# Last attention pair: block transfers over two queues with diagonal copies on GpSimd, one head weighted on ScalarE, maxima exchanged in another PSUM bank

## The chip, the cores and the metric

The kernel runs on one core of one Trainium2 chip. The metric is device microseconds of one execution; a kernel's time is the median of several. Engines are named as the profile names them: PE (TensorE matmul), PEld (its weight load), DVE (VectorE), ACT (ScalarE), POOL (GpSimd), SP (SyncE, which here only issues transfers); SPq and ACTq are the transfers that SP and ACT issue.

## The reference

Two layers over 512 tokens of width 1024: an attention mixer, a gated feed-forward, an mLSTM mixer and another feed-forward. The change touches the attention mixer alone. It has 8 heads of width 128 and three groups of queries, keys and values (window and dilation 128/1, 512/4, 2048/16):

```python
for g, (window, dilation) in enumerate(DIL_CONFIGS):
    q = apply_partial_rope(proj[:, :, g, 0], positions) * scale
    k = apply_partial_rope(proj[:, :, g, 1], positions)
    v = proj[:, :, g, 2]
    o, lse = dilated_window_attention(q, k, v, window, dilation)   # softmax within a group
    ...
wts = jax.nn.softmax(jnp.stack(lses), axis=0)                      # softmax over the groups
o = jnp.einsum('gbsh,gbshd->bshd', wts.astype(xn.dtype), jnp.stack(outs))
return o.reshape(B, S, ATTN_WIDTH) @ w_out
```

## The kernel before

All products of float32 data are made of three matmuls: each operand is split into a high part (ACT, names ending in `_h`) and a rest (DVE, `_l`), and high x high, low x high and high x low are summed in PSUM. PE runs nearly without a break through the whole program, and the other engines prepare its operands.

Attention goes by pairs of heads (`attention_pair(pr)`, pr 0 to 3; tiles of pair 3 begin with `a3`, those of pair 2 with `a2`; pair 3 is heads 6 and 7). Each pair has these steps:

- projections of q and k, then `scores0` and `scores12`: scores, masks with row maxima on DVE, exponentials on ACT. The result for head i is tile `p[i]` (`a3p`), 15 blocks of 128x128.
- `joint`: the groups hold their tokens in two orders, so each row's maximum and sum must be brought to the other order. `exchange` does this with one matmul into a PSUM tile `xps` (`a3xps`). `joint` then makes the weights `cf` (`a3cf`).
- `weigh(i)`: eight multiplications of blocks of `p[i]` by a column of `cf`, on DVE.
- `transposes(i)`: one DVE instruction transposes all 32x32 blocks within `p[i]` into `t` (`a3pB`). What is left of a 128x128 transpose is to move block row b of partition group a to block row a of group b.
- For pairs 0 to 2 that move goes through DRAM on POOL's queue (`bring(i)`), hidden behind the next pair. For pair 3 (`end`) there is no next pair: 16 transfers a head of 32x480 go straight from `a3pB` to `a3pT`, head 6's alternately on ACT and SP, head 7's all on SP.
- `values(i)`: 30 recorded matmuls of `a3pT` with the values give the head's output in PSUM (`a3o`), which is split into `ao_h` and `ao_l` for the output projection.

PSUM tiles come from four tags, each a ring of buffers: "s" (2), "o" (2), "acc" (3) and "t" (1). Scores, `xps` and the heads' outputs use "o". A tile waits until the one that held its buffer has been read.

The last pair's work is interleaved by hand with the output projection (`awo`, in four column chunks c of 256, each in two row chunks `_k0` and `_k1`); `run` keeps the PE instructions of a step together and in order. On PE the order is: `awo` chunk 0, scores of pair 3, chunk 1, head 4's values (`a2o`), the exchange, head 5's values, chunk 2, then the parts of all chunks that need heads 4 and 5, head 6's values between the second and the third of them, head 7's values, and the parts that need heads 6 and 7. The weights of chunk 2's second row chunk are split on ACT (L207) and DVE (L208) behind the transfers that ACT issues.

Of the kernel before, what the change touches and what calls it, by code (L numbers as in the profile page):

```python
# [11 lines left out]
F32 = mybir.dt.float32  # L12
F32R = mybir.dt.float32r
I32 = mybir.dt.int32
AF = mybir.ActivationFunctionType
ALU = mybir.AluOpType
AX = mybir.AxisListType
P = 128
# [5 lines left out]
HEADS = 8  # L24
# [46 lines left out]
def tile_hybrid_dilated_attn_mlstm(  # L71
# [4 lines left out]
    nc = tc.nc  # L76
# [3 lines left out]
    def pool(stack, name, **kw):  # L80
        return stack.enter_context(tc.tile_pool(name=name, bufs=1, **kw))
# [4 lines left out]
    ps = pool(ctx, "psum", space=bass.MemoryType.PSUM)  # L86
# [51 lines left out]
    def defer(n, fn):  # L138
        later.append((tick[0] + n, next(order), fn))
# [36 lines left out]
    def fenced():  # L176
        return tc.issue_after(fence[0]) if fence[0] is not None else nullcontext()

    def acc_tile(name):
        return ps.tile([P, 512], F32, tag="acc", name=name, bufs=3)  # L180
# [163 lines left out]
    with ExitStack() as actx:  # L344
# [3 lines left out]
        R = 32  # L348
# [12 lines left out]
        ang, n, sn, cs = (boot[:, 0, i * P:(i + 1) * P] for i in range(4))  # L361
# [28 lines left out]
        def tok_tile(name):  # L390
            return ap.tile([P, 2, SEQ], F32, tag="qk", name=name, bufs=6)
# [16 lines left out]
        xps = {}  # L408
# [286 lines left out]
        def columns(c0):  # L695
# [4 lines left out]
                            lambda i, tb, n=n: v_all[1 + n][i][tb]) for n in range(2)]  # L700
# [35 lines left out]
        def o_head(k):  # L736
            return v_all[0][:, :, k * P:(k + 1) * P]

        def attention_pair(pr):
            nm = "a%d" % pr  # L740
# [7 lines left out]
            end = pr == HEADS // 2 - 1  # L748
            pts, vt, weight = {}, [], []

            def score_bank(i, name):
                return ps.tile([P, 512], F32, tag="so"[i], name=name, bufs=2)
# [23 lines left out]
            def scores12(qk1, qk2):  # L776

                for i in range(2):
                    for g, (q, k) in ((1, qk1), (2, qk2)):
                        sp = score_bank(i, "%ss%d" % (nm, g))  # L780
                        for c in range(4):
                            sl = slice(c * P, (c + 1) * P)
                            nc.tensor.matmul(sp[:, sl], q[:, i, sl], k[:, i, sl], start=True, stop=True)
                        for c in range(4):
                            sl = slice(c * P, (c + 1) * P)
                            nc.vector.tensor_tensor_reduce(
                                p12[i][:, 4 * (g - 1) + c, :], sp[:, sl], mask_causal if g == 1 else mask_dil,
                                1.0, -3e38, op0=ALU.add, op1=ALU.max, accum_out=mx[:, g - 1, i, c:c + 1])
                    exponentials(1, i)
# [20 lines left out]
            def exchange():  # L810

                ex = ap.tile([P, 2, 2, 2, 4, 4], F32, tag="ex", name=nm + "ex")
                for st in range(2):
                    nc.vector.tensor_tensor(
                        ex[:, st].rearrange("p o i b c -> p (o i b) c"),
                        own[:, st].rearrange("p o i b -> p (o i b)").unsqueeze(2).to_broadcast([P, 16, 4]),
                        mask_part.unsqueeze(1).to_broadcast([P, 16, 4]), op=ALU.mult)
                xps = ps.tile([P, 512], F32, tag="o", name=nm + "xps", bufs=2)
                nc.tensor.matmul(xps[:, :P], perm, ex.rearrange("p s o i b c -> p (s o i b c)"), start=True, stop=True)
                ex2 = ap.tile([P, 8, 4, 4], F32, tag="ex2", name=nm + "ex2")  # L820
                nc.vector.tensor_tensor(
                    ex2, xps[:, :P].rearrange("p (s b c) -> p s c b", b=4, c=4),
                    mask_part.unsqueeze(1).unsqueeze(1).to_broadcast([P, 8, 4, 4]), op=ALU.mult)
                ex4 = ex2.rearrange("p (s o i) c b -> p s o i c b", s=2, o=2)
                for o in range(2):
                    nc.vector.tensor_reduce(oth[:, :, 1 - o], ex4[:, :, o], axis=AX.X, op=ALU.add)
# [18 lines left out]

            def weigh(i):
                cf4 = weight[0]
                for b in range(4):
                    pb = max(2 * b - 1, 0)
                    blk = p0[i][:, pb:2 * b + 1, :].rearrange("p a b -> p (a b)")  # L850
                    nc.vector.tensor_scalar(blk, blk, cf4[:, 0, i, b:b + 1], None, op0=ALU.mult)
                for c in range(4):
                    blk = p12[i].rearrange("p (g c) k -> p c g k", g=2)[:, c]
                    nc.vector.tensor_scalar(blk, blk, cf4[:, 1, i, c:c + 1], None, op0=ALU.mult)

            def transposes(i):


                t = ap.tile([P, 4, 15, R], F32, tag="p", name=nm + "pB", bufs=3)
                nc.vector.transpose(t.rearrange("p b n i -> p n b i"), p[i])  # L860
                if end:
                    pt = pts[i] = ap.tile([P, 4, 15, R], F32, tag="pt", name=nm + "pT", bufs=2)
                    for n in range(16):
                        a, b = n // 4, n % 4
                        (nc.sync if n % 2 or i else nc.scalar).dma_start(pt[R * b:R * (b + 1), a], t[R * a:R * (a + 1), b])
                    return
                d = pts[i] = dp.tile([4, R, 4, 15 * R], F32, tag="d", name=nm + "pD", bufs=2)
                for a in range(4):
                    nc.gpsimd.dma_start(d.rearrange("b j a x -> a j b x")[a],
                                    t[R * a:R * (a + 1)].rearrange("p b n i -> p b (n i)"))  # L870

            def bring(i):
                if end:
                    return
                pt = ap.tile([P, 4, 15, R], F32, tag="pt", name=nm + "pT", bufs=2)
                nc.gpsimd.dma_start(pt.rearrange("p a n i -> p (a n i)"), pts[i].rearrange("b j a x -> (b j) (a x)"))
                pts[i] = pt
# [20 lines left out]
            qks = []  # L898
            for g in range(3):
# [3 lines left out]
                for part in range(2):  # L903
                    t = tok_tile("%sg%d_%s" % (nm, g, "qk"[part]))
# [30 lines left out]
                    values_stage()  # L935
                if g == (2 if pr == 0 else 0):
                    defer(1 if pr == 0 else RUN_AT[0], lambda: run(lambda: scores0(*qks[0])))
            turn = ((lambda: weigh(0), lambda: transposes(0), lambda: bring(0), lambda: weigh(1), lambda: transposes(1),
                     lambda: bring(1)) if pr == HEADS // 2 - 1 else
                    (lambda: weigh(0), lambda: transposes(0), lambda: weigh(1), lambda: transposes(1),  # L940
                     lambda: bring(0), lambda: bring(1)))
            later_runs = ((lambda: scores12(*qks[1:]),), (joint, *turn))
            if pr < 2:
                later_runs += ((lambda: values(0), lambda: values(1)),)
            v1 = v_all[1 + pr // 2]
            vt.extend(lambda c, i, g=g: v1[g][c][:, (pr % 2 * 2 + i) * P:(pr % 2 * 2 + i + 1) * P] for g in range(2))
            if pr == HEADS // 2 - 1:
                return [lambda fns=fns: run(*fns) for fns in later_runs], values
            for at, fns in zip(RUN_AT[1:], later_runs):
                defer(at, lambda fns=fns: run(*fns))  # L950
# [4 lines left out]
        for pr in range(HEADS // 2):  # L955
            last_runs, values_of = attention_pair(pr)
# [5 lines left out]
        def heads_split(*ks):  # L962
            for k in ks:
                split_act(blocks4(pair[0][k]), blocks4(pair[1][k]), o_head(k), None)
# [7 lines left out]
        def out_project(pairs, w2d, nk, name, first=0, end=KC // 2):  # L972
            for c in range(first, end):
# [2 lines left out]

        assert not later
        acc = [[acc_tile("awo0_%d" % m) for m in range(2)],
               [ps.tile([P, 512], F32, tag="s", name="awo1_%d" % m, bufs=2) for m in range(2)],
               [acc_tile("awo2_0"), ps.tile([P, 512], F32, tag="t", name="awo2_1", bufs=1)]]  # L980

        def out_part(c, whl, ch, ks=None, last=False):
            for m in range(2):
                with fenced():
                    multiply(acc[c][m], whl, pair, ch, m, KC, ks)
                if last:
                    add_to_h(c)(m, acc[c][m])

        def out_weights(c, ch):
            return split_chunk(weight_chunk(attn_w_out[0], ch, c * 256, 4, "awo%d_k%d" % (c, ch)))  # L990
# [5 lines left out]
        last_runs[1]()  # L996
        run(lambda: early_values(1))
        heads_split(4, 5)
        out_part(2, out_weights(2, 0), 0)
        whl = [out_weights(c, 1) for c in range(3)]  # L1000
        for c in range(2):
# [500 lines left out]
    with ExitStack() as mctx:  # L1502
        mp = pool(mctx, "mlstm")
        H = HEADS
        blk = lambda t: t.rearrange("p (b s) -> p b s", b=TB)
# [50 lines left out]
        for p_ in (0, 32):  # L1556
            s = slice(p_, p_ + H)
# [46 lines left out]
        for b in range(TB):  # L1604
            ve.scalar_tensor_tensor(fblk[32 * b:32 * b + H], blk(lf)[:, b], bias2[:, 1:2], blk(t0)[:, b],
                                    op0=ALU.add, op1=ALU.add)
# [14 lines left out]
        for b in range(TB):  # L1621
            s = slice(32 * b, 32 * b + H)
# [16 lines left out]
        i = 0  # L1639
        for kb in range(TB):  # L1640
            for qb in range(kb, TB):
                pidx[kb, qb] = i
                to = brow[kb][:, qb - kb]
# [282 lines left out]
```

## Time and profile before

| what | value |
|---|---|
| timed runs | 1417.63, 1417.75, 1419.54 us; median 1417.75 |
| the profiled execution's own time | 1419.82 us |
| its span, first to last instruction | 1417.7 us |
| mean granted TensorE clock | 0.995 |
| PE, DVE, ACT, POOL busy | 98%, 77%, 48%, 8% of the span |
| HBM read and written | 162.19 MB and 10.09 MB |

In timelines each row has the start and the length in us, the engine, the line, the operation with the tile it writes and those it reads, a count, and in brackets the time for which the engine stood idle before it and what ended that. In the chain of work that ended last each row is a start, a length and what ran. A row of a stretch has busy times of PE, PEld, DVE, ACT and POOL with instruction counts, then the granted TensorE clock (1.00 is full speed), the mean busy share of the 16 DMA engines, and GB/s. Rows of one line's instructions give durations in ns as least/median/most.

### The profile page before, as it was taken

The numbers are of one execution on the slowest core, as the hardware profiler recorded it, in microseconds if no ns is written. First come the engines' busy times: TensorE is split into PE (matmuls) and PEld (weight loads), VectorE is DVE, ScalarE is ACT, GpSimd is POOL, SyncE is SP. The second block draws the span as 40 slices with busy tenths as digits, with TensorE's granted clock in tenths as the row PEclk, the third lists the DMA queues.
The fourth block names the chain that finished last, engine by engine and source line by source line (L and its number), as shares of the span: only waits on it lengthen the run. The fifth ranks groups of instructions, "written<-read, shape, count | busy, mean of one in ns | idle before, by whom it ended". The sixth has DMA issues, their size and how long they took to land.

```text
span 1417.7 us, 20912 instructions
## 1 busy us (share of the span) xinstructions
PE 1394.7 (98%) x8118; PEld 1230.2 (87%) x8118; DVE 1090.2 (77%) x1850; ACT 673.7 (48%) x1111; POOL 108.9 (8%) x153
## 2 busy tenths in 40 slices
PE   9999999999999899999999999999999999999997
PEld 7788888888888788999999988798888899998886
DVE  7976659687797487787898678987748778789775
ACT  7245553232333343444574553785534344457434
POOL 1014101000010000000011010000000000001222
PEclk9999999999999999999999999999999999999999
DMA  9538634427262324323576442221132432337762
GB/s 300 145 76 221 170 106 115 155 81 238 75 215 79 97 90 134 112 68 119 149 213 149 87 119 82 69 88 61 60 104 89 134 107 73 120 120 206 179 136 74
DMA packets 134763, 177.71 MB, mean 125 GB/s; under 512 B 7876, under 2 KB 99332, under 8 KB 134664
## 3 DMA queue, kind: packets, MB, share of 16 engines
q1 hardware_dynamic: 118896, 140.89, 31.9%
q0 software_dynamic: 13728, 33.86, 11.5%
q10 hardware_dynamic: 2040, 1.61, 0.4%
q8 instruction: 64, 1.05, 0.3%
q14 instruction: 35, 0.29, 0.1%
HBM read 162.19 MB, written 10.09 MB: 122 GB/s over the span
## 4 chain that ended last, share of the span: by engine, by line
PE 83%; DVE 10%; ACT 3%; issue 2%; DMA 1%; SPq 1%; ACTq 0%; DVEq 0%
PE f0j_u L1199 5%; PE f1j L238 5%; PE f0j L238 5%; PE f1j_u L1199 4%; PE f0j_p L1199 3%; PE f0j_c L1199 3%; PE mwo L238 3%; PE f1j_c L1199 3%; PE f1j_p L1199 3%; PE mo L238 3%; PE o_o L1451 2%; PE o_o L1854 2%; PE awo L238 2%; PE o_acc L1868 2%; PE o_s L1451 2%; PE o_acc L1451 2%
## 5 line engine op out<-in xcount | busy, mean ns | idle before, releaser
L238 PE MATMUL f1j<-n_h,f1j_h 128*128 128x512 f32 x96 | 37.5, 390 | 0.0
L238 PE MATMUL f0j<-n_h,f0j_h 128*128 128x512 f32 x96 | 37.5, 390 | 0.0
L238 PE MATMUL f1j<-n_h,f1j_l 128*128 128x512 f32 x96 | 37.4, 389 | 0.0
L238 PE MATMUL f0j<-n_h,f0j_l 128*128 128x512 f32 x96 | 37.4, 389 | 0.0
L238 PE MATMUL f0j<-n_l,f0j_h 128*128 128x512 f32 x96 | 37.3, 389 | 0.0
L238 PE MATMUL f1j<-n_l,f1j_h 128*128 128x512 f32 x96 | 37.3, 389 | 0.0
L1297 POOL DMA_DIRECT2D o0own<-in_ffn_w_out_dram x8 | 10.3, 1302 | 331.2 <-PE f0j_u L1199 288.8
L1297 POOL DMA_DIRECT2D o1own<-in_ffn_w_out_dram x8 | 9.8, 1276 | 287.2 <-DVE o1B L1343 258.3
L523 DVE TENSOR_TENSOR rot<-rot,sinr 32x1024 f32<-32x1024 f32 x24 | 28.9, 1205 | 0.0
L238 PE MATMUL mqk<-n_h,mqk_k_h 128*128 128x512 f32 x64 | 25.7, 402 | 0.0
L238 PE MATMUL mqk<-n_h,mqk_k_l 128*128 128x512 f32 x64 | 25.7, 401 | 0.0
L238 PE MATMUL mqk<-n_l,mqk_k_h 128*128 128x512 f32 x64 | 25.5, 398 | 0.0
L238 PE MATMUL mo<-n_h,mo_k_h 128*128 128x512 f32 x64 | 25.4, 397 | 0.0
L238 PE MATMUL mo<-n_h,mo_k_l 128*128 128x512 f32 x64 | 25.2, 394 | 0.0
L238 PE MATMUL mo<-n_l,mo_k_h 128*128 128x512 f32 x64 | 25.2, 394 | 0.0
L238 PE MATMUL awo<-ao_h,awo_k_h 128*128 128x512 f32 x64 | 25.1, 395 | 0.0
L238 PE MATMUL awo<-ao_l,awo_k_h 128*128 128x512 f32 x64 | 25.1, 392 | 0.0
L238 PE MATMUL awo<-ao_h,awo_k_l 128*128 128x512 f32 x64 | 25.0, 391 | 0.0
L238 PE MATMUL mwo<-yo_h,mwo_k_h 128*128 128x512 f32 x64 | 24.9, 389 | 0.0
L238 PE MATMUL mwo<-yo_l,mwo_k_h 128*128 128x512 f32 x64 | 24.9, 389 | 0.0
L238 PE MATMUL mwo<-yo_h,mwo_k_l 128*128 128x512 f32 x64 | 24.9, 389 | 0.0
L208 DVE TENSOR_TENSOR o1a_l<-o1a_w,o1a_h 128x1024 fp32r<-128x1024 f32 x12 | 14.7, 1223 | 12.6 <-ACT o1a_h L207 12.6
(2321 smaller groups left out, 5426.3 us busy)
## 6 DMA issues: line engine op xcount, KB each, us to landing
f0j_w<-in_ffn_w_in_dram SPq DMA_DIRECT2D x28, 512.0 KB, 4.2
f1j_w<-in_ffn_w_in_dram SPq DMA_DIRECT2D x28, 512.0 KB, 3.9
o0a_w<-in_ffn_w_out_dram SPq DMA_DIRECT2D x12, 512.0 KB, 4.1
o1a_w<-in_ffn_w_out_dram SPq DMA_DIRECT2D x12, 512.0 KB, 8.4
awo_k_w<-in_attn_w_out_dram SPq DMA_DIRECT2D x8, 512.0 KB, 4.7
o0own<-in_ffn_w_out_dram POOLq DMA_DIRECT2D x8, 512.0 KB, 9.7
mv_k_w<-in_mlstm_w_in_dram SPq DMA_DIRECT2D x8, 512.0 KB, 3.9
mqk_k_w<-in_mlstm_w_in_dram SPq DMA_DIRECT2D x8, 512.0 KB, 3.6
```

The lines of the kernel that those rows point to most:

```text
L208: nc.vector.tensor_tensor(lo[:, :n], raw[:, :n], hi[:, :n].bitcast(F32), op=ALU.subtract)
L238: nc.tensor.matmul(acc, whl[a][:, k, m * P:(m + 1) * P], pairs[b][kk], start=(kk == 0 and (a, b) == SPLITS[0]), stop=(kk == nk - 1 and (a, ...
L523: nc.vector.tensor_tensor(sh, sh, sinr.unsqueeze(1).to_broadcast([R, 2, SEQ]), op=ALU.mult)
L1199: nc.tensor.matmul(acc[name][:, m * HALF:(m + 1) * HALF], whl[a][:, k, m * P:(m + 1) * P], ops[okey][b][:, k], start=(fresh and m == 0 and ...
L1297: nc.gpsimd.dma_start(view, self.source(col, ch), accum_op=ALU.add)
L1451: nc.tensor.matmul(dst[m // 2][:, (m % 2) * HALF:(m % 2 + 1) * HALF], whl[a][:, k, m * P:(m + 1) * P], unit.form(okey, b, 2 * c + k), star ...
L1854: nc.tensor.matmul(dst[t], unit.form(okey, a, 2 * c + k)[:, t * P:(t + 1) * P], whl[b][:, k], start=(first and k == 0 and (a, b) == SPLITS ...
L1868: nc.tensor.matmul(rest[n][tb], unit.plain[c][a][k][:, tb * P:(tb + 1) * P], whl[b][:, k], start=(c == 0 and (n == 1 or tb >= 2) and k == ...
```

## The change

For the last pair alone:

- `xps` is taken from tag "t" instead of "o"; the accumulator `awo2_1`, which also lives in "t", is created later, after the exchange.
- `weigh(1)` (head 7) runs on ACT instead of DVE.
- Of each head's 16 transfers the four diagonal ones (a = b) become copies on POOL; the other twelve alternate between SP and ACT for both heads, so each queue issues six a head.
- `weigh(1)` and `transposes(1)` become a step of their own, run after head 5's values and their split.

```diff
-                xps = ps.tile([P, 512], F32, tag="o", name=nm + "xps", bufs=2)
+                xps = ps.tile([P, 512], F32, tag="ot"[end], name=nm + "xps", bufs=2 - end)
...
+                def scale(blk, by):
+                    if end and i:
+                        nc.scalar.activation(blk, blk, AF.Copy, scale=by)
+                    else:
+                        nc.vector.tensor_scalar(blk, blk, by, None, op0=ALU.mult)
...
-                    nc.vector.tensor_scalar(blk, blk, cf4[:, 0, i, b:b + 1], None, op0=ALU.mult)
+                    scale(blk, cf4[:, 0, i, b:b + 1])
...
-                    for n in range(16):
-                        a, b = n // 4, n % 4
-                        (nc.sync if n % 2 or i else nc.scalar).dma_start(pt[R * b:R * (b + 1), a], t[R * a:R * (a + 1), b])
+                    for a, b in itertools.product(range(4), repeat=2):
+                        to, of = pt[R * b:R * (b + 1), a], t[R * a:R * (a + 1), b]
+                        if a == b:
+                            nc.gpsimd.tensor_copy(to, of)
+                        else:
+                            (nc.sync, nc.scalar)[(a + b + (a > b)) % 2].dma_start(to, of)
...
+                later_runs = ((lambda: scores12(*qks[1:]),), (joint, lambda: weigh(0), lambda: transposes(0)),
+                              (lambda: weigh(1), lambda: transposes(1)))
...
-               [acc_tile("awo2_0"), ps.tile([P, 512], F32, tag="t", name="awo2_1", bufs=1)]]
...
         run(lambda: early_values(1))
         heads_split(4, 5)
+        last_runs[2]()
+        acc.append([acc_tile("awo2_0"), ps.tile([P, 512], F32, tag="t", name="awo2_1", bufs=1)])
```

On DVE, from the last step of `joint` to the second transpose, the order before (`a3p_2857` is head 6, `a3p_2858` head 7; `ao_l_3434` is the rest of heads 4 and 5):

```order
L843 TENSOR_TENSOR a3cf<-a3cf,a3ee 128x16
L851 TENSOR_SCALAR a3p_2857<-a3p_2857,a3cf 128x128
L851 TENSOR_SCALAR a3p_2857<-a3p_2857,a3cf 128x256 x3
L854 TENSOR_SCALAR a3p_2857<-a3p_2857,a3cf 128x2x128 x4
L851 TENSOR_SCALAR a3p_2858<-a3p_2858,a3cf 128x128
L860 STREAM_TRANSPOSE a3pB<-a3p_2857 128x15x4x32
L851 TENSOR_SCALAR a3p_2858<-a3p_2858,a3cf 128x256 x3
L854 TENSOR_SCALAR a3p_2858<-a3p_2858,a3cf 128x2x128 x4
L223 TENSOR_TENSOR ao_l_3434<-v_763,ao_h_3433 128x512
L860 STREAM_TRANSPOSE a3pB<-a3p_2858 128x15x4x32
```

and the order now at the same place:

```order
L843 TENSOR_TENSOR a3cf<-a3cf,a3ee 128x16
L853 TENSOR_SCALAR a3p_2857<-a3p_2857,a3cf 128x128
L853 TENSOR_SCALAR a3p_2857<-a3p_2857,a3cf 128x256 x3
L853 TENSOR_SCALAR a3p_2857<-a3p_2857,a3cf 128x2x128 x4
L223 TENSOR_TENSOR ao_l_3434<-v_763,ao_h_3433 128x512
L866 STREAM_TRANSPOSE a3pB<-a3p_2857 128x15x4x32
L866 STREAM_TRANSPOSE a3pB<-a3p_2858 128x15x4x32
```

Head 7's eight multiplications have left DVE, the two transposes stand next to each other, and head 5's `ao_l` has moved ahead of the first.

On ACT, from `joint`'s exponential to the split of the weights behind the transfers, before:

```order
L838 ACTIVATE a3ee<-a3ee 128x32
L894 ACTIVATE v_763<-a2o 128x4x128
L222 ACTIVATE ao_h_3433<-v_763 128x512
L865 DMA a3pT<-a3pB 32x480 x8
L207 ACTIVATE awo_k_h<-awo_k_w 128x1024
```

and now (`a3p_2858` is head 7):

```order
L838 ACTIVATE a3ee<-a3ee 128x32
L851 ACTIVATE a3p_2858<-a3p_2858,a3cf 128x128
L901 ACTIVATE v_763<-a2o 128x4x128
L851 ACTIVATE a3p_2858<-a3p_2858,a3cf 128x256
L222 ACTIVATE ao_h_3433<-v_763 128x512
L851 ACTIVATE a3p_2858<-a3p_2858,a3cf 128x256 x2
L851 ACTIVATE a3p_2858<-a3p_2858,a3cf 128x2x128 x4
L874 DMA a3pT<-a3pB 32x480 x12
L207 ACTIVATE awo_k_h<-awo_k_w 128x1024
```

Head 7's multiplications stand between and behind the copy and the split of head 5's output, and twelve transfers instead of eight stand ahead of the split of the weights. SP issues twelve of these transfers instead of 24, and POOL's queue has eight copies where it had nothing between pair 2's transfers and the feed-forward's loads. On PE one wait changes: head 5's values no longer wait for ACT's copy of head 4's output.

More of the change, by code (lines that the diff above doesn't have):

```diff
@@ L850, in weigh @@
                     blk = p0[i][:, pb:2 * b + 1, :].rearrange("p a b -> p (a b)")
-                    nc.vector.tensor_scalar(blk, blk, cf4[:, 0, i, b:b + 1], None, op0=ALU.mult)
+                    scale(blk, cf4[:, 0, i, b:b + 1])
                 for c in range(4):
                     blk = p12[i].rearrange("p (g c) k -> p c g k", g=2)[:, c]
-                    nc.vector.tensor_scalar(blk, blk, cf4[:, 1, i, c:c + 1], None, op0=ALU.mult)
+                    scale(blk, cf4[:, 1, i, c:c + 1])
             def transposes(i):
@@ L872, in bring @@
             def bring(i):
-                if end:
-                    return
                 pt = ap.tile([P, 4, 15, R], F32, tag="pt", name=nm + "pT", bufs=2)
@@ L937, in attention_pair @@
                     defer(1 if pr == 0 else RUN_AT[0], lambda: run(lambda: scores0(*qks[0])))
-            turn = ((lambda: weigh(0), lambda: transposes(0), lambda: bring(0), lambda: weigh(1), lambda: transposes(1),
-                     lambda: bring(1)) if pr == HEADS // 2 - 1 else
-                    (lambda: weigh(0), lambda: transposes(0), lambda: weigh(1), lambda: transposes(1),
+            if end:
+                later_runs = ((lambda: scores12(*qks[1:]),), (joint, lambda: weigh(0), lambda: transposes(0)),
+                              (lambda: weigh(1), lambda: transposes(1)))
+            else:
+                later_runs = (
+                    (lambda: scores12(*qks[1:]),),
+                    (joint, lambda: weigh(0), lambda: transposes(0), lambda: weigh(1), lambda: transposes(1),
                      lambda: bring(0), lambda: bring(1)))
-            later_runs = ((lambda: scores12(*qks[1:]),), (joint, *turn))
             if pr < 2:
@@ L946, in attention_pair @@
             vt.extend(lambda c, i, g=g: v1[g][c][:, (pr % 2 * 2 + i) * P:(pr % 2 * 2 + i + 1) * P] for g in range(2))
-            if pr == HEADS // 2 - 1:
+            if end:
                 return [lambda fns=fns: run(*fns) for fns in later_runs], values
@@ L978, in tile_hybrid_dilated_attn_mlstm @@
         acc = [[acc_tile("awo0_%d" % m) for m in range(2)],
-               [ps.tile([P, 512], F32, tag="s", name="awo1_%d" % m, bufs=2) for m in range(2)],
-               [acc_tile("awo2_0"), ps.tile([P, 512], F32, tag="t", name="awo2_1", bufs=1)]]
+               [ps.tile([P, 512], F32, tag="s", name="awo1_%d" % m, bufs=2) for m in range(2)]]
         def out_part(c, whl, ch, ks=None, last=False):
```

## The prediction

> **What bounds the kernel now.** I read the page's first part, then TensorE's waits, the chain that ended last, and TensorE's timeline around the longest wait.
>
> ```profile
> PE 1394.7 (98%) x8118; PEld 1230.2 (87%) x8118; DVE 1090.2 (77%) x1850; ACT 673.7 (48%) x1111; POOL 108.9 (8%) x153
> ```
> ```profile
> PE a3o L885 <- DMA a3pT<-a3pB: 4.0, 1, 4.0
> ...
> PE a2o L885 <- ACT v L894: 0.5, 1, 0.5
> ```
>
> TensorE is the bound, 98% of the span, so only time in which it stands still or runs slowly can be won. Its longest single wait, 4.0 us, is for the transfers of the last pair, and one of 0.5 us lies in the same stage. The chain (start, us, what) shows why.
>
> ```profile
> 453.98 2.10 DVE a3pB L860
> 456.13 0.60 SPq L865
> ...
> 460.90 0.60 SPq L865
> 461.75 0.51 SPq L865
> ...
> 471.38 1.97 DMA a3pT<-a3pB
> ```
> ```profile
> L865 SPq DMA_DIRECT2D a3pT<-a3pB x24: 507/589/831, 456.1 to 471.4; - x24
> L865 ACTq DMA_DIRECT2D a3pT<-a3pB x8: 601/607/615, 456.1 to 460.6; - x8
> DMA to landing us min/median/max: 1.9/2.0/2.3
> ```
>
> SP issues 24 transfers one behind the other, 0.66 us apart (15.25 us over 23 steps), ACT eight at 0.64 us. Head 6's eight on SP end with the one at 460.90; head 7's sixteen begin at 461.75, all on SP, and the last lands 1.97 us after 471.38, at 473.35. What that does to TensorE:
>
> ```profile
> 448.65 1.83 PE L885 MATMUL a2o<-a2pT,v 128*128 128x128 f32 x14 [0.46 <-ACT v L894]
> 463.25 1.72 PE L885 MATMUL a3o<-a3pT,v 128*128 128x128 f32 x14
> 466.51 0.48 PE L238 MATMUL awo<-ao_h,awo_k_h 128*128 128x512 f32 x1
> 468.91 0.39 PE L238 MATMUL awo<-ao_l,awo_k_h 128*128 128x512 f32 x1
> 469.14 0.39 PE L238 MATMUL awo<-ao_h,awo_k_l 128*128 128x512 f32 x1
> 473.55 3.33 PE L885 MATMUL a3o<-a3pT,v 128*128 128x128 f32 x14 [4.02 <-DMA a3pT<-a3pB]
> 479.82 0.48 PE L238 MATMUL awo<-ao_h,awo_k_h 128*128 128x512 f32 x1
> ```
>
> The same 30 matmuls take 466.51-463.25 = 3.26 us for head 6 and 479.82-473.55 = 6.27 us for head 7, behind the wait. The stretches tell why (PE, PEld, DVE, ACT and POOL busy, then granted clock, DMA share, GB/s):
>
> ```profile
> 456.00:463.00 7.00, 7.00 (x31) 5.55 (x30) 5.16 (x11) 1.06 (x1) 0.00 (x0) 1.00 0.61 144
> 463.00:469.20 6.20, 6.20 (x44) 5.60 (x42) 1.33 (x2) 0.60 (x1) 0.00 (x0) 1.00 0.41 97
> 472.80:473.50 0.70, 0.00 (x0) 0.00 (x0) 0.00 (x0) 0.00 (x0) 0.00 (x0) 0.55 0.35 57
> 473.50:480.00 6.50, 6.45 (x31) 6.49 (x32) 0.00 (x0) 0.00 (x0) 0.00 (x0) 0.52 0.25 80
> 909.50:910.00 0.50, 0.50 (x3) 0.46 (x4) 0.30 (x2) 0.00 (x0) 0.00 (x0) 0.78 0.00 0
> 910.00:911.00 1.00, 1.00 (x5) 0.90 (x5) 1.00 (x3) 0.00 (x0) 0.00 (x0) 0.50 0.00 0
> 913.00:913.50 0.50, 0.50 (x3) 0.39 (x2) 0.50 (x1) 0.50 (x4) 0.00 (x0) 0.80 0.00 0
> ```
>
> In the wait the granted clock falls to half, and head 7's product runs at 0.52. A second stretch at half clock lies from about 909.8 to 913.2, far from the change.
>
> **The change part by part.** Gains first.
>
> (a) *Exchange in bank "t".* The wait of 0.46 us goes: the next product no longer needs ACT's copy out of the second "o" bank. The product also started slower behind it (1.83 against 1.72). Gain 0.5. Both ends: 0 (something else holds it) to 0.6.
>
> (b) *The wait for head 7.* TensorE's pitch is 0.23 us (468.91 to 469.14), so the product could start at 469.37; it started at 473.55: 4.18 us.
>
> (c) *The half clock.* 6.27-3.26 = 3.01 us. TensorE: Matmul & The Clock Gate (the Trainium skill), "What's actually happening", says that full rate returns after some 3.4 us of sustained work; by that rule half of 3.4, 1.7 us, would be an estimate of this term, and the sum 6.4 instead of 7.7. The trace differs here (6.3 us at half clock) and agrees at 910 (some 3.4 us). I take 3.01, the row of this very place.
>
> Sum: 0.5+4.18+3.01 = 7.7 us, if nothing new makes TensorE wait. That needs four arrivals checked.
>
> ```profile
> 451.67 1.07 DVE L851 TENSOR_SCALAR a3p<-a3p,a3cf 128x128 f32<-128x128 f32 x4
> 453.71 0.28 DVE L851 TENSOR_SCALAR a3p<-a3p,a3cf 128x128 f32<-128x128 f32 x1
> 453.90 2.17 DVE L860 STREAM_TRANSPOSE a3pB<-a3p 128x1920 f32<-128x1920 f32 x1
> 457.80 0.68 DVE L223 TENSOR_TENSOR ao_l<-v,ao_h 128x512 fp32r<-128x512 f32 x1
> 458.40 2.17 DVE L860 STREAM_TRANSPOSE a3pB<-a3p 128x1920 f32<-128x1920 f32 x1
> 462.41 1.23 DVE L208 TENSOR_TENSOR awo_k_l<-awo_k_w,awo_k_h 128x1024 fp32r<-128x1024 f32 x1 [1.84 <-ACT awo_k_h L207]
> ```
> ```profile
> 452.31 0.60 ACT L894 ACTIVATE v<-a2o 128x512 f32<-128x512 f32 x1 [1.68 <-PE a2o L890]
> 452.94 0.63 ACT L222 ACTIVATE ao_h<-v 128x512 fp32r<-128x512 f32 x1
> 461.32 1.06 ACT L207 ACTIVATE awo_k_h<-awo_k_w 128x1024 fp32r<-128x1024 f32 x1 [7.75 <-DMA a3pT<-a3pB]
> ```
> ```profile
> L800 ACT ACTIVATE a3p<-a3p,a3nb x8: 382/494/497, 403.6 to 413.3; 128x256 f32<-128x256 f32 x6, 128x128 f32<-128x128 f32 x2
> ```
> ```profile
> L388 POOL COPY boot<-boot 32x128 f32<-32x128 f32 x4 | 1.1, 285 | 0.2
> ```
> ```profile
> L1676 POOL CAST ql<-ql x8: 610/611/1128, 891.2 to 949.4; 64x512 fp32r<-64x512 f32 x8
> ```
>
> (d) *Head 7 weighted on ACT.* No scaling on ACT is in the trace; the nearest rows are exponentials of the same shapes, 0.38 us (128x128) and 0.49 (128x256), which also take a column per partition. Back to back I take 0.40. ACT: one scaling from 451.67, the copy v from 451.97 (its product now ends about 451.8), a second scaling, then the split ao_h to about 453.5, six more scalings to 456.0. DVE ends head 6's weights at 453.71, does head 5's ao_l (a step of 0.60: 457.80 to 458.40), which now stands ahead of the first transpose, and transposes head 6 from 454.3 to 456.5 (0.4 later than now) and head 7 to 458.7 (1.9 earlier). If a scaling took 0.3 or 0.6, head 7's transpose, which waits for all eight, would end at 458.7 or 459.4.
>
> (e) *Six transfers a queue and head.* Head 6: from 456.5, five steps of 0.64 to 0.70 and 2.0 to land: 461.9, at most 462.3. Its product is asked for at 463.25-0.5 = 462.7: slack 0.4 to 0.8. Head 7: six more steps, last landing at 465.8 to 466.5; asked for at 469.37-0.5 = 468.9: slack 2.4 at least. So both transfers' cost is hidden by TensorE's own work; were it gone, every us would show. SP then frees its queue by 464.5 instead of 472, so f0j_w is loaded earlier; nobody waits for that now: 0.
>
> (f) *Diagonal copies on POOL*, four a head of 32x480, on a queue that has nothing else here. A straight line through 0.285 (128 columns) and 0.611 (512) gives 0.58; ends 0.285 and 1.13 (the slower casts). With 0.58, head 6's end at 458.8 and head 7's at 461.2; with 1.13 at 461.0 and 465.5. Both in time: 0.
>
> (g) *ACT's queue.* ACT now issues twelve, 456.5 + 12 x 0.64 = 464.2, and behind them stands the split awo_k_h, now at 461.32, of the weights that TensorE wants at 466.51-0.5 = 466.0. It would end at 465.25, its rest on DVE (1.23) at 466.5; TensorE's order now takes four matmuls (0.9 us) before it needs that rest, 466.9. Slack 0.4 to 0.75: cost 0, but the thinnest cover of all. At 0.83 us an issue (the slowest SP row) it would end at 467.5, with the rest at 468.8: a wait of about 1.9 us.
>
> The profiled execution took 1419.82 us (its span is 1417.7, with 2.1 around it), so 1412.1 by its own time. It stands 2.1 above the median of the timed runs, 1417.75. The half clock at 910, some 3.4 us long and so worth 1.7, would be most of that if the quicker runs lack it; then they would give 1410.4, and 1417.75-7.7 is 1410.05. I forecast 1410.5.
>
> **The rivals.**
>
> 1. *ACT's queue is late (g), or head 6's transfers are (e).* For it: slacks of 0.4 us. Against: every step is priced by a row of the same stage. It costs up to 1.9 us: 1411.5 to 1413.
>
> 2. *The transfers don't get faster.* DMA: Bandwidth & Descriptors (the Trainium skill), "Issuing engines are not separate DMA queues", says that all transfers run on the same 16 engines, and that a second issuer saves only issue time. As a mechanism here: if 0.65 us were the engines' pace and not the queue's, 24 transfers from 456.5 would last to 472.1 and land at 474, after 473.55; head 6's twelve would land at about 466, 3.3 us late. Gains (a) to (c) would then be gone: about 1418, no change. Against it: with both queues issuing, 16 transfers went out in 5.4 us (to 461.5), and the engines were busy 0.61 of the time (0.41 behind it).
>
> 3. *Slower: POOL's copies are the bound.* Eight in a row must be done by 468.9, so from 1.55 us each TensorE waits again. From 2.1 us each (456.5+8x2.1 = 473.3) head 7 is as late as now and the gain is gone; at 2.6 us it starts at 477.3, and at half clock ends at 483.6 instead of 479.82: 1417.75+3.8-0.5 = 1421. SBUF — State Buffer (the Trainium skill), "Who interferes with whom", speaks for it: GpSimd shares its ports with VectorE, and the loser waits out the whole instruction. Against it: one 2.17 us transpose is all that DVE runs beside them, and no row of a copy is above 1.13.
>
> 4. *The drop of the clock costs less in the timed runs than in the profiled one* (1.7 instead of 3.01): 1411.4. It changes the size alone.
>
> **How the numbers follow.** 0.2% is 2.8 us, about what a measurement of this kernel can tell from no change. Forecast with 4, both waits gone: 0.82, at 1409 to 1412.5. Rival 1: 0.10. Rival 2: 0.05. Rival 3: 0.03. The range, 1408.8 to 1413.3, holds the forecast, most of rival 1 and both states of the stretch at 910. Below 1414.9 lie the forecast and nearly all of rival 1: faster 0.91; same 0.06 (rival 2 and the weak end of 1); slower 0.03.
>
> **What would show it.** In the changed trace TensorE's waits hold neither a3o<-a3pT nor a2o<-v; head 7's product takes 3.3 us from about 469 and the clock there is 1.00; SP's twelve issues end by 464.5; each POOL copy takes 0.3 to 1.1 us; awo_k_h on ACT ends by 465.3. I am wrong if a3o or awo still waits over 1 us between 462 and 470, if the copies pass 1.5 us, or if the clock still falls.

## The result, and the profile after

| | before | after |
|---|---|---|
| median of the timed runs | 1418.49 us | 1410.18 us |
| least and most | 1417.05, 1420.11 (6 runs) | 1409.88, 1410.85 (6 runs) |
| the profiled execution's own time | 1419.82 | 1410.27 |
| its span | 1417.7 | 1408.5 |

The ratio is 0.9942, with a 95% interval of 0.9929 to 0.9955: 8.3 us faster (6.4 to 10.1), at 1410.18 where 1410.5 was forecast. Held against before's medians in the three later groups, all near 1417.7, the gain is 7.3 to 7.6 us. Two single runs of later kernels, of 2308 and 7906 us, lie far from all others of their kernels for a reason that the record does not show, and are left out below.

The page's first part for the kernel after:

```profile
PE 1390.5 (99%) x8118; PEld 1226.5 (87%) x8118; DVE 1088.0 (77%) x1842; ACT 676.8 (48%) x1119; POOL 113.8 (8%) x161
```

TensorE's longest waits after (us in total, times, longest) contain neither a3o nor a2o:

```profile
PE o_o L1462 <- DVE hx L1492: 1.8, 2, 1.3
PE idle L107 <- DVE idle_w L102: 1.5, 1, 1.5
PE m1nb L1696 <- ACT m0e L1706: 1.0, 1, 1.0
```

The chain of work that ended last (start, length, what) is now TensorE alone in this stage; the pieces of SP's queue and of the DMA are gone from it:

```profile
463.20 1.71 PE a3o L892 x14
464.90 1.79 PE a3o L897 x16
466.69 2.87 PE awo L238 x12
...
```

TensorE's timeline after, at the places that were shown of before. In this execution the whole stage starts 0.72 us later (its first a2o matmul at 445.18, before at 444.46), so 0.72 is taken off where a time is held against the prediction.

```profile
448.75 1.73 PE L892 MATMUL a2o<-a2pT,v 128*128 128x128 f32 x14
463.10 1.80 PE L892 MATMUL a3o<-a3pT,v 128*128 128x128 f32 x14
466.44 0.48 PE L238 MATMUL awo<-ao_h,awo_k_h 128*128 128x512 f32 x1
467.45 0.48 PE L238 MATMUL awo<-ao_h,awo_k_l 128*128 128x512 f32 x1
469.40 1.72 PE L892 MATMUL a3o<-a3pT,v 128*128 128x128 f32 x14
472.66 0.48 PE L238 MATMUL awo<-ao_h,awo_k_h 128*128 128x512 f32 x1
```

No row has an idle time in brackets. Head 7's product takes 472.66-469.40 = 3.26 us, what head 6's took before. From the first a2o matmul to the first awo behind head 7's product the stage takes 27.48 us; before it took 479.82-444.46 = 35.36. The difference, 7.88, stands against a predicted sum of 7.7. The rest of the span went from 1382.34 to 1381.02, 1.32 less, though nothing in it was changed: a stretch at half clock, worth 1.7 us, is missing there. The stretches (busy times of PE, PEld, DVE, ACT, POOL, granted clock, DMA share, GB/s) show full clock both here and around 910, where the trace of before had 3.4 us at half:

```profile
456.00:463.00 7.00, 7.00 (x32) 5.63 (x30) 3.39 (x2) 0.59 (x2) 4.67 (x8) 1.00 0.52 122
469.00:473.00 4.00, 4.00 (x35) 3.87 (x34) 0.00 (x0) 0.06 (x1) 0.00 (x0) 1.00 0.35 121
906.00:914.00 8.00, 8.00 (x38) 6.50 (x37) 8.00 (x13) 6.70 (x11) 0.00 (x0) 1.00 0.40 110
```

The transfers and copies, from the view of tile a3pT (durations in ns as least/median/most, first and last start in us):

```profile
L874 ACTq DMA_DIRECT2D a3pT<-a3pB x12: 514/606/612, 457.2 to 464.4; - x12
L874 SPq DMA_DIRECT2D a3pT<-a3pB x12: 507/593/829, 457.3 to 464.7; - x12
L872 POOL COPY a3pT<-a3pB x8: 578/583/590, 457.3 to 461.7; 32x480 f32<-32x480 f32 x8
...
DMA to landing us min/median/max: 1.9/2.0/2.3
```

On each queue the twelfth issue starts 6.7 us before the last of SP's 24 did (471.4; 7.4 us with the 0.72 taken off), at nearly the same pace (0.65 and 0.67 us against 0.64 and 0.66) and with the same landing time. The timelines of DVE and ACT after:

```profile
452.39 2.13 DVE L853 TENSOR_SCALAR a3p<-a3p,a3cf 128x128 f32<-128x128 f32 x8
455.04 4.46 DVE L866 STREAM_TRANSPOSE a3pB<-a3p 128x1920 f32<-128x1920 f32 x2
466.16 1.23 DVE L208 TENSOR_TENSOR awo_k_l<-awo_k_w,awo_k_h 128x1024 fp32r<-128x1024 f32 x1 [6.67 <-ACT awo_k_h L207]
```
```profile
454.10 2.49 ACT L851 ACTIVATE a3p<-a3p,a3cf 128x256 f32<-128x256 f32 x6
465.07 1.06 ACT L207 ACTIVATE awo_k_h<-awo_k_w 128x1024 fp32r<-128x1024 f32 x1 [8.48 <-DMA a3pT<-a3pB]
```

### The profile page after: what moved, and what is told of

The parts are those of the page before. It is cut to its first block, busy times and chain, and to the rows that moved or that the text cites. A ratio compares the mean times of both kernels' runs of the same rounds, so it can differ in the third digit from the quotient of the medians.

```text
span 1408.5 us, 20915 instructions
## 1 busy us (share of the span) xinstructions
PE 1390.5 (99%) x8118; PEld 1226.5 (87%) x8118; DVE 1088.0 (77%) x1842; ACT 676.8 (48%) x1119; POOL 113.8 (8%) x161
## 3 DMA queue, kind: packets, MB, share of 16 engines
q8 instruction: 64, 1.05, 0.3%
## 4 chain that ended last, share of the span: by engine, by line
PE 85%; DVE 10%; ACT 3%; issue 2%; DMA 1%; ACTq 0%; DVEq 0%
PE f0j_u L1210 5%; PE f1j L238 5%; PE f0j L238 5%; PE f1j_u L1210 4%; PE f0j_p L1210 3%; PE f0j_c L1210 3%; PE awo L238 3%; PE mwo L238 3%; PE f1j_c L1210 3%; PE f1j_p L1210 3%; PE mo L238 3%; PE o_o L1462 2%; PE o_o L1865 2%; PE o_acc L1879 2%; PE o_s L1462 2%; PE o_acc L1462 2%
```

## The experiments

My theory was the sum of the prediction: the transfers' issue on SP alone made head 7 late (4.18 us), the wait made the clock fall (3.01), and the bank gave 0.5. The rivals were that the gain came from the bank or from ACT's weighting; that the DMA engines and not the queue set the pace; and that copies on POOL have a price. "Stage" below is the length defined above, always of the one profiled execution: 35.36 us before, 27.48 after. The kernels ran in three groups, in which before's median was 1417.70 (21 runs), 1417.77 (20) and 1417.68 (15).

**The transfers alone**, in before:

```diff
-                    for n in range(16):
-                        a, b = n // 4, n % 4
-                        (nc.sync if n % 2 or i else nc.scalar).dma_start(...)
+                    for a, b in itertools.product(range(4), repeat=2):
...
+                        if a == b:
+                            nc.gpsimd.tensor_copy(to, of)
+                        else:
+                            (nc.sync, nc.scalar)[(a + b + (a > b)) % 2].dma_start(to, of)
```

> The kernel before with only the transfers changed: diagonal blocks copied on GpSimd, the other twelve of each head alternating between SP and ACT. Theory (the one SP queue was the whole cost): head 7's last block lands near 466.5 us against 469.4 when it is asked for, so the 4.0 us wait and the half clock behind it go; the 0.46 us wait for the o bank stays. About 7.2 us less than before (ratio 0.995), PE waits for a3pT 0. Rival (the three parts are needed together, since head 7's transpose still ends at 460.6 and not at 458.7): a wait of 1 to 2 us is left, 5 to 6 us less than before.

Measured: 1413.48 us (1411.35 to 1414.77, four runs), ratio 0.9965 (0.9951 to 0.9978); stage 29.57, 5.8 better, in the quickest of the four. The 7.2 expected were missed. The rival's figure of 5 to 6 was met, but not by the wait it named: the wait for head 7 and the half clock are gone, and TensorE has a new wait, in its timeline:

```profile
459.79 0.50 PE L238 MATMUL awo<-ao_l,awo_k_h 128*128 128x512 f32 x1 [1.32 <-DVE ao_l L223]
```

DVE is late with ao_l, because head 7's scalings stand ahead of it and have become slower. Its timeline, with POOL's beside it (in before the same seven took 0.83 and 1.13 us):

```profile
455.81 1.55 DVE L851 TENSOR_SCALAR a3p<-a3p,a3cf 128x256 f32<-128x256 f32 x3
457.28 1.85 DVE L854 TENSOR_SCALAR a3p<-a3p,a3cf 128x256 f32<-128x256 f32 x4
```
```profile
456.00 2.46 POOL L866 COPY a3pT<-a3pB 32x480 f32<-32x480 f32 x4 [48.74 <-DVE a3pB L860]
```

By single instructions (tile a3p, two stretches of 0.7 us; durations in ns) the scalings that start beside a copy take 0.70 us, the others 0.31 to 0.34:

```profile
L851 DVE TENSOR_SCALAR a3p<-a3p,a3cf x2: 701/701/701, 456.0 to 456.7; 128x256 f32<-128x256 f32 x2
L854 DVE TENSOR_SCALAR a3p<-a3p,a3cf x2: 704/707/710, 457.3 to 457.9; 128x256 f32<-128x256 f32 x2
```

There are four copies and four scalings of 0.70: 4 x 0.36 = 1.44 us, which is all of 0.72 + 0.72. The transfers are not what slows them: in the next run, with transfers on both queues and no copies, the same seven take what they took in before:

```profile
455.73 0.84 DVE L851 TENSOR_SCALAR a3p<-a3p,a3cf 128x256 f32<-128x256 f32 x3
456.48 1.14 DVE L854 TENSOR_SCALAR a3p<-a3p,a3cf 128x256 f32<-128x256 f32 x4
```

So the transfers carry the gain, and the copies on POOL do cost something: not on POOL, but on DVE. Why two of the four runs took 3 us more than the profiled one stays open.

**Two queues without POOL**, in before: all sixteen stay DMAs.

```diff
-                        (nc.sync if n % 2 or i else nc.scalar).dma_start(...)
+                        (nc.sync if n % 2 else nc.scalar).dma_start(...)
```

> The kernel before with all 16 transfers of head 7 alternating between SP and ACT as head 6's do; no copies on GpSimd. Theory (ACT's queue is the thinnest cover): the blocks land near 468, in time, but ACT issues sixteen, to 466.5, so the split of the weights behind them ends near 467.6 and its rest on VectorE near 468.8, and TensorE waits for these 1.5 to 2 us in all; 5 to 5.5 us less than before (ratio 0.9963). Rival (the queue is all that matters, ACT's split is hidden): 7.2 us less, as with the copies. Rival (the diagonal copies carry the gain): under 3 us less.

Measured: 1412.85 us (1412.44 to 1413.28, five runs), ratio 0.9961 (0.9949 to 0.9974); stage 29.82, 5.5 better, as expected. Head 7 has no wait, so 32 transfers on two queues are quick enough: the DMA engines were not the limit. What comes instead is the thin cover of step (g), ACT's sixteen issues ahead of the split of the weights:

```profile
467.52 0.50 PE L238 MATMUL awo<-ao_h,awo_k_h 128*128 128x512 f32 x1 [1.02 <-ACT awo_k_h L207]
```

The copies on POOL thus aren't needed for the transfers; they take four issues a head off the queues, two of them off ACT. In transfers_alone, which has them, ACT's split ended at 466.75, ahead of the 467.72 at which TensorE took it.

**ACT's weighting alone**, in before (`scale` for head 7 as in the change, transfers as before):

> The kernel before with only head 7's weights taken to ACT. Theory: head 7's transpose ends 2.5 us earlier, near 458, but its transfers stand behind head 6's on SP to 461.5 anyway, so they land as late as before: 0 to 0.4 us less than before, the wait for a3pT is still about 4 us and the clock still falls. Rival (DVE's weighting was on the path to the wait): 2 us less.

**The bank alone**, in before (`xps` in "t", `awo2_1` created after the exchange):

> The kernel before with only the exchange moved to bank t. Theory: TensorE's wait of 0.46 us for the o bank goes, but the blocks of head 7 land at the same time, so the wait for them grows from 4.0 to about 4.5 us and the total stays: 0.0 us, ratio 1.000. Rival (the sum of the parts holds one by one): 0.5 us less.

Measured: 1416.82 us (1416.29 to 1419.07, ten runs), ratio 0.9996 (0.9987 to 1.0005), and 1417.67 (1417.16 to 1419.87, eleven runs), ratio 1.0000 (0.9991 to 1.0009). Neither alone moves the time beyond its interval. Their stages, 34.05 and 33.83, are 1.3 and 1.5 shorter than in before's profile, but that is the clock: these two executions had 3.41 us at half behind the wait and not 6.82, and head 7's product took 4.98 and 4.72 instead of 6.27. TensorE's timelines show why nothing else is gained; of ACT's weighting, then of the bank:

```profile
474.15 2.81 PE L891 MATMUL a3o<-a3pT,v 128*128 128x128 f32 x14 [3.90 <-DMA a3pT<-a3pB]
```
```profile
473.77 3.17 PE L885 MATMUL a3o<-a3pT,v 128*128 128x128 f32 x14 [4.23 <-DMA a3pT<-a3pB]
```

The wait for head 7's transfers is still there, and with the bank it has grown from 4.02 to 4.23 (about 4.5 was expected; another 0.15 now goes to a wait for ao_l, at 458.75): what TensorE saves ahead of a late transfer it spends waiting.

**The bank undone**, in after:

```diff
-                xps = ps.tile([P, 512], F32, tag="ot"[end], name=nm + "xps", bufs=2 - end)
+                xps = ps.tile([P, 512], F32, tag="o", name=nm + "xps", bufs=2)
```

> The changed kernel with the exchange back in bank o. Theory: with nothing late behind it the wait of 0.46 us before head 5's values is paid in full: 0.4 to 0.6 us above the changed kernel (about 1410.7). Rival (the bank is worth nothing): the same as the changed kernel, 1410.2.

Measured: 1411.02 us (1410.49 to 1411.2, five runs), ratio 0.9946 (0.9932 to 0.996); stage 27.95. The wait is back, and costs 0.47 now that hardly anything behind it is late:

```profile
449.36 1.83 PE L892 MATMUL a2o<-a2pT,v 128*128 128x128 f32 x14 [0.46 <-ACT v L901]
```

**ACT's weighting undone**, in after (`scale` back to `nc.vector.tensor_scalar`):

> The changed kernel with head 7 weighted on VectorE again. Theory: head 7's transpose ends near 460.6 instead of 458.7 on the time scale of the kernel before, SP and ACT issue its blocks right then (they are free of head 6's at 460.4), the last lands near 466; nothing waits: the same as the changed kernel within 0.3 us. Rival (the weighting on ACT is a part of the gain): 1 to 2 us above it.

Measured: 1412.0 us (1411.7 to 1414.16, five runs), ratio 0.9959 (0.9946 to 0.9972); stage 29.09, so 1.6 us worse: the rival's 1 to 2 us, and not the theory's 0.3 at most. The timelines of TensorE and DVE:

```profile
467.83 0.50 PE L238 MATMUL awo<-ao_h,awo_k_h 128*128 128x512 f32 x1 [1.11 <-ACT awo_k_h L207]
```
```profile
457.17 1.72 DVE L851 TENSOR_SCALAR a3p<-a3p,a3cf 128x128 f32<-128x128 f32 x4
458.81 1.85 DVE L854 TENSOR_SCALAR a3p<-a3p,a3cf 128x256 f32<-128x256 f32 x4
460.69 2.18 DVE L860 STREAM_TRANSPOSE a3pB<-a3p 128x1920 f32<-128x1920 f32 x1
```

The eight scalings take 3.6 us beside POOL's copies, where head 6's eight, just ahead and without copies, took 2.2 (1.08 and 1.14). So head 7's transpose ends at 462.9 and not at 461.4, ACT issues until 466.6, and the split of the weights behind those issues starts at 466.73, 1.7 later than in after. By this reckoning there would have been next to no wait had the scalings kept their pace. Head 5's ao_l stands ahead of these scalings here (the new step for head 7 puts it there), so the wait for it that transfers_alone had is absent and the delay shows at the weights. That step has no run of its own; after_old_transfers below contains it. As in transfers_alone, two of the runs took some 2 us more than the others, which stays open.

**The transfers undone**, in after:

> The changed kernel with the old transfers (sixteen a head, head 7's all on SP, no GpSimd copies). Theory: the first transpose ends 0.4 us later than before and SP is as slow as before, so head 7's last block lands near 473.7; the wait is near 5 us, the clock falls, and the time is that of the kernel before within 0.5 us. Rival (the earlier transpose of head 7 is worth its 2 us): 2 us less than before.

Measured: 1419.56 us (1417.29 to 1420.5, eleven runs), ratio 1.0005 (0.9996 to 1.0014); stage 35.47. All the gain is gone, with the bank, the new step and ACT's weighting still in. Both heads wait, 5.1 us in all where near 5 was expected:

```profile
463.35 1.80 PE L889 MATMUL a3o<-a3pT,v 128*128 128x128 f32 x14 [0.91 <-DMA a3pT<-a3pB]
...
473.91 3.32 PE L889 MATMUL a3o<-a3pT,v 128*128 128x128 f32 x14 [4.20 <-DMA a3pT<-a3pB]
```

**Each copy on POOL three times**, in after, to try rival 3's point of decision:

```diff
-                            nc.gpsimd.tensor_copy(to, of)
+                            for _ in range(3):
+                                nc.gpsimd.tensor_copy(to, of)
```

> The changed kernel with each diagonal copy on GpSimd issued three times (the same result). Theory (a copy takes 0.58 us, 0.62 us from start to start, and the cover ends at 1.55 us a copy for head 6 and head 7): twelve copies take 7.5 us a head, so head 6's blocks are complete 1.3 us after TensorE asks for them and head 7's again 1.3 us late: 2.3 to 2.9 us above the changed kernel (about 1412.8), with PE waiting for POOL twice. Rival (GpSimd's copies are slowed by VectorE's transposes, or hidden whatever they take): over 5 us above, or the same as the changed kernel.

Measured: 1416.24 us (1415.13 to 1417.95, eleven runs), ratio 0.9988 (0.9979 to 0.9997); stage 33.42, 5.9 worse than after. TensorE's timeline, and POOL's copies in two stretches from the view of tile a3pT:

```profile
464.56 1.83 PE L893 MATMUL a3o<-a3pT,v 128*128 128x128 f32 x14 [1.77 <-POOL a3pT L873]
...
473.21 3.22 PE L893 MATMUL a3o<-a3pT,v 128*128 128x128 f32 x14 [2.29 <-POOL a3pT L873]
```
```profile
L873 POOL COPY a3pT<-a3pB x8: 577/581/586, 459.5 to 463.9; 32x480 f32<-32x480 f32 x8
...
L873 POOL COPY a3pT<-a3pB x2: 578/1083/1588, 465.8 to 467.5; 32x480 f32<-32x480 f32 x2
```

The mechanism is as rival 3 had it: once the copies are the last to arrive, TensorE waits for POOL. My figure, about 1412.8, was missed; 5.9 is in the range of the expectation's rival, "over 5 us", though not by its cause, since the copies beside the transposes kept their 0.58. Two points were left out. One copy took 1.59 us instead of 0.58: it ran while DVE had its 1.23 us TENSOR_TENSOR on the weights (from 465.76), so the cost between POOL and DVE falls on either of them. And the second wait, only 2.29 us long, made the clock fall: 3.42 us at half, worth 1.7. The waits and the clock together, 1.77 + 2.29 + 1.7 = 5.8, are the 5.9.

**TensorE kept warm in before's wait**: 17 matmuls of 128x512 on data that is there, into head 7's own bank, ahead of its product, which overwrites them.

```diff
+                for _ in range(17 if end and i else 0):
+                    nc.tensor.matmul(op, ones_r, pair_ao[0][0], start=True, stop=True)
                 first = True
```

> The kernel before with 17 matmuls of 128x512 that multiply constants into head 7's own PSUM bank, ahead of its product (which overwrites them): TensorE is busy for about 3.9 of the 4.2 us of the wait. The blocks land when they did. Theory: the clock does not fall, head 7's product takes 3.3 instead of 6.3 us, and the kernel takes about 3.0 us less than before (ratio 0.998) though the wait for the data is as long. Rival (the slow product is not the clock's doing, but late data within it): no change.

Measured: 1415.64 us (1414.52 to 1417.71, eleven runs), ratio 0.9982 (0.9973 to 0.9991); stage 32.35.

```profile
469.69 4.13 PE L885 MATMUL a3o<-ao_h,ones_r 128*128 128x512 f32 x17
473.81 1.80 PE L889 MATMUL a3o<-a3pT,v 128*128 128x128 f32 x14
```

The product starts no earlier (473.81), yet the stage is 3.01 us shorter, because the clock stays full (1.00 from 469 to 480). This is term (c) by itself, to the hundredth in these two executions. Over all runs it is less: the medians differ by 2.0, and the ratio gives 2.6 (1.3 to 3.8), since many of before's runs, by their clock, do not pay the whole 3.01 (see (c) below).

**After once more**, on another chip than the first two groups:

> The changed kernel itself, for comparison on the same chip: 7.7 to 8.3 us less than before. Theory on the scatter: its runs agree within 1 us, where those of the kernel before differ by 3, because the half-clock stretches of the latter (behind the wait, and near 910 us) vary from run to run. Rival: the scatter is the chip's, and the changed kernel's runs scatter as widely here.

Measured: 1410.43 us (1409.97 to 1411.01, five runs), ratio 0.9948 (0.9935 to 0.996), stage 27.45. By the medians that is 7.25 less than before, a little short of the 7.7 to 8.3 expected. The runs lie within 1.04 us and before's beside them within 3.9, so the scatter is not the chip's.

## Why the prediction was right

- *(a) The bank*: 0.5 predicted, 0.47 measured, but only with the transfers changed too; alone it is worth nothing. The 0.47 is net: from the first a2o matmul to head 5's product it saves 0.62 (448.75-445.18 = 3.57 in after, 449.36-445.17 = 4.19 in after_o_bank), and the arrivals at (e) and (g) take some of it back.
- *(b) The wait for head 7*: gone, and by the stated cause. The transfers alone take it away; the other two parts don't.
- *(c) The half clock*: 3.01 predicted and 3.01 measured, in the profiled executions; warm_before, which removes this term alone, is the test of it. Rival 4 holds for other executions: act_alone, bank_alone and copies_thrice paid for only 3.4 us at half. Before's runs accordingly lie in two groups, for the most part from 1416.3 to 1418.2 at a mean clock of 0.997 or 0.998 and from 1419.0 to 1420.1 at 0.994 to 0.996, while after's eleven stay within 1.2 us. TensorE: Matmul & The Clock Gate (the Trainium skill), "What's actually happening", gives full rate back after a busy window of about 3.4 us. By that rule the prediction estimated 1.7 for this term, and set it aside for the row's 3.01; the trace agrees with the length of the window, and the row of 3.01 holds two of them (6.82 us at half, below).
- *The level*: before's profiled execution less the stage's gain and less the 1.7 at 910 was forecast as 1410.4; after's has 1410.27. The step that the quicker runs lack the stretch at 910 fits after's profiles, all of which lack it. That the second way, 1417.75-7.7 = 1410.05, came out too is partly luck: it takes the profiled execution's 3.01 off a median run that probably paid less, and three more runs moved that median to 1418.49.
- *(d) Head 7 weighted on ACT*: the scalings take 2.49 us for six, 0.415 each, against 0.40. (The trace of before did have scalings on ACT, n_h at L225, of 128x512; none of these shapes.) What I mis-sized is what the part is worth. I costed it only by when the transposes end; the sum has no term for it, and I expected 0.3 us at most from undoing it. Undoing it cost 1.6 us: on DVE these scalings would run beside POOL's copies and take 3.6 us instead of 2.2.
- *(e) The transfers*: the last issue starts at 464.7 and lands 2.0 later, less 0.72 at 466.0, in the forecast 465.8 to 466.5. Rival 2 is refuted by two_queues. For head 6 the slack of 0.4 to 0.8 was not there. The matmul at 462.81 plus the pitch of 0.23 puts the request at 463.04, on the prediction's scale 462.3 and not 462.7, and SP's sixth issue, at 460.8, lands near 462.8. The product starts 0.06 late and loses 0.08 more in its first steps (3.34 us against 3.26). PEld stood idle for 0.30 us before its weight load at 463.07, for a reason that the profile does not name; in after_o_bank, 0.6 us behind, the hold is absent.
- *(f) The copies*: 0.58 interpolated, 0.583 measured, and cost 0 in after. That is so only because DVE ran nothing but the transposes beside them, which lose little: the two take 4.46 us there, where one took 2.17 in before. SBUF — State Buffer (the Trainium skill), "Who interferes with whom", has tensor_scalar in VectorE's two-port modes block against GpSimd, and an instruction with two SBUF inputs against GpSimd's reads. The trace agrees with both: 0.70 against 0.34 for a scaling, 1.59 against 0.58 for a copy. The argument against rival 3, that one transpose is all that runs beside the copies, was right for this kernel; the prediction did not see that part (d) is what makes it so.
- *(g) ACT's queue*: the thinnest cover indeed, and thinner than said. The rest of the weights ends at 466.16 + 1.23 = 467.39 and TensorE takes it at 467.45: no slack of 0.4, but a first matmul of 0.48 us whose successor follows after 0.33 instead of 0.23, so 0.1 us is lost. In after_o_bank, with TensorE 0.6 later, the same matmul takes 0.39 and loses nothing. So rival 1 came true by some 0.2 us, here and at (e). awo_k_h ended at 466.13, less 0.72 at 465.4 against 465.25, and TensorE asked for the rest 0.2 earlier than worked out. With four more issues on ACT (two_queues) the wait is there.

## What to carry to other kernels

When a wait ends with a run of small transfers, look at the pace of their issue (here 0.66 us each, 24 on one queue) before anything else: spreading them over idle queues and engines won the wait, and the clock that falls behind it. An operation moved to GpSimd is not free because GpSimd is idle: list what VectorE runs beside it, since here 2.3 us of copies cost VectorE 1.4, and moving that work away was the part that looked superfluous. A saving ahead of a late arrival shows nothing alone, so parts of a change should also be tried by undoing them from the whole.

## What the hardware showed beyond this

The half-clock stretches within the work all last one or two times 3.41 us. Of before, around its two stretches (columns as above):

```profile
472.48:472.88 0.40, 0.00 (x0) 0.00 (x0) 0.00 (x0) 0.00 (x0) 0.00 (x0) 0.99 0.59 139
472.88:479.70 6.82, 6.15 (x29) 6.18 (x30) 0.00 (x0) 0.00 (x0) 0.00 (x0) 0.50 0.26 80
...
909.78:913.20 3.42, 3.42 (x11) 2.79 (x11) 3.22 (x8) 2.16 (x9) 0.00 (x0) 0.50 0.00 0
913.20:913.60 0.40, 0.40 (x4) 0.31 (x3) 0.40 (x2) 0.40 (x3) 0.00 (x0) 1.00 0.00 0
```

The second stretch begins in the middle of busy work, 0.41 us behind the last idle piece. The two starts fit a grid: (909.78-472.88)/128 = 3.4133 us. Laid over an execution from any one of its edges, a grid of this period meets the others; its phase differs from execution to execution. The stretch near 910 follows two short idle pieces. They are in before and after alike (in after 1.04 us until 900.30 and 0.75 until 902.23), and what decides, by the table, is whether one window holds both. Counting TensorE's idle time in each window, with after's grid taken from where its clock falls behind the last matmul, at 1403.38:

| execution | window | idle in it, us | the window behind it |
|---|---|---|---|
| before, after_old_transfers | ends 909.78, 909.54 | 1.78 | half |
| warm_before | ends 907.32 | 1.59 | half |
| copies_thrice | ends 466.57 | 1.41 | full |
| act_alone | ends 908.21 | 1.33 | full |
| after | ends 901.63 | 1.19 | full |
| copies_thrice | ends 473.39 | 2.29 | half |
| before (at half) | ends 476.29 | 0.67 | stays half |
| bank_alone (at half) | ends 476.66 | 0.53 | full again |

All windows of the twelve profiled executions, up to the last matmul and not only these, fit a limit between 1.41 and 1.59 us of idle time in a window, and a lower one, 0.53 to 0.67, for coming back. So here a wait of 2.3 us cost 1.7 more (copies_thrice), and two waits of 1.05 and 0.73 that fell into one window cost the same (before). This was fitted to the traces and not tried by a run of its own. Open is why the stretch is missing from all profiles with the gain: by the limit and the lengths of the pieces some 3 phases in 10 should show it, as 3 of the 6 profiles without the gain did. Six profiles would all miss it by chance one time in eight (0.7^6 = 0.12); the narrow scatter of after's eleven runs suggests that they miss it too, but most of them have no trace.
